# The opening of a two-layer decoder trunk: token statistics by single-column products, c as one row, other orders of transfer

## The chip, the cores and the metric

The kernel runs on one core of a Trainium2 chip. The core has a tensor engine (PE, with its weight loads shown apart as PEld), VectorE (DVE), ScalarE (ACT), GpSimd (POOL) and SyncE (SP), which here only issues transfers. Each works through its own queue in order, and they meet through semaphores. The metric is the device time of one execution in microseconds (us), the median of several runs.

## The reference

Two layers; in each an adaptive layer norm, a mixer block and a feed-forward block. What matters here is the very start:

```python
c_act = jax.nn.silu(c)                                   # c: (1, 1024)
mod = (c_act @ w_ada + b_ada)[:, None, :]                # six parts of 1024
sh1, sc1, g1, sh2, sc2, g2 = jnp.split(mod, 6, axis=-1)
h = rmsnorm(x, norm1_w) * (1 + sc1) + sh1                # x: (1, 512, 1024) f32
u = h @ w_in
...
def rmsnorm(x, w):
    xf = xf * lax.rsqrt(jnp.mean(xf * xf, axis=-1, keepdims=True) + EPS)
    return xf.astype(x.dtype) * w
```

All is fp32. The mean runs over the 1024 features of each of the 512 tokens.

## The kernel before

Activations lie with features on partitions: `x[k]`, k = 0 to 7, is a tile of 128 features by 512 tokens. A product of full accuracy is three products of split operands (`mm3`, L156): each operand is split into a rounded part `hi`, made on ScalarE, and the rest `lo`, made on DVE. Weights arrive by SyncE as `raw` tiles (`fetch`, L229), ScalarE makes `whi` (L322) and DVE makes `wlo` (L325).

**The opening.** ScalarE's queue loads c, already spread over 128 partitions by the host (512 KB, L184), and the columns `colt`; SyncE loads the eight x tiles (256 KB each, L187) and behind them, per tile k, the weights of the scale part SC1 and of the shift part SH1 (512 KB each, `ada_first_load`, L374), then `raw` tiles. A dot of such weights with `csil`, the silu of c, is one DVE pass over 128x1024 (`ada_dot`, L371); ScalarE turns its sum into a column of `amod` or `mod` (L388, L391).

For the statistics DVE and ScalarE square the x tiles (L725, L727), DVE adds them in pairs (L729), and PE multiplies each pair's sum by a tile of ones (L730), which leaves the sum over features in all 128 partitions, 128x512. The root comes from ScalarE (L737) and three DVE passes over 128x512 improve it by a newton step (L738 to L740) into `norm.rstd`.

**The first input tiles.** Tile k of h is made in three steps: `first_scaled` (x times scale column times rstd, DVE, L490), `first_hi` (plus shift column, rounded, ScalarE, L494) and `first_lo` (DVE, L497). With `hi`, `lo`, `whi` and `wlo` of tile k PE does 21 products of 512 columns for that k (L787, L789); k runs from 0 to 7 with seven sums open at once. From k=2 on, the step for k+2 is written ahead of the products of k.

**What sets the order.** `pin` and `matmul` keep DVE's and PE's instructions in the order of the code. ScalarE's and SyncE's are placed by the scheduler that builds the program, by its own idea of when operands are there. Products of ones by ones (`WARM`, 22 of them, at the start; `WARM2`, 16, ahead of the main work) have no result that is used.

Of the kernel before, what the change touches and what calls it, by code (L numbers as in the profile page):

```python
# [12 lines left out]
F32 = mybir.dt.float32  # L13
F32R = mybir.dt.float32r
I32 = mybir.dt.int32
AF = mybir.ActivationFunctionType
ALU = mybir.AluOpType
# [3 lines left out]
P = 128  # L21
D = 1024
S = 512
L = 2
KT = D // P
# [3 lines left out]
TT = S // P  # L29
# [5 lines left out]
BLOCK = 256  # L35
DFF = 2816
NF = DFF // P
EPS = 1e-6
# [18 lines left out]
SH1, SC1, G1, SH2, SC2, G2 = range(6)  # L57
# [9 lines left out]

WARM = 22

WARM2 = 16  # L70

GATE2 = ([("gate", j) for j in range(6)] + [("attn", 0), ("attn", 1), ("gate", 6), ("gate", 7)]
         + [("attn", j) for j in range(2, 8)])
# [3 lines left out]
def hybrid_trunk(ctx, tc, xT, ws, ada, cols, pool_w, qk_w, crow, pos, con, out):  # L77
    nc = tc.nc
    V, A, T = nc.vector, nc.scalar, nc.tensor
# [14 lines left out]
    def bigt(dt=F32R):  # L94
        return big.tile([P, S], dt, tag="big", name=nm("big"))
# [4 lines left out]
    def ps_mm():  # L100
        return psum.tile([P, S], F32, tag="mm", name=nm("mm"), bufs=4)
# [7 lines left out]
    def sm(shape, dt=F32, tag="sm", bufs=8):  # L109
        return small.tile(shape, dt, tag=tag, name=nm(tag), bufs=bufs)  # L110
# [36 lines left out]
    def matmul(*a, **k):  # L147
        tc.keep_in_program_order(T.matmul(*a, **k))  # L148

    def pin(ins):  # L150
        return tc.keep_in_program_order(ins)
# [16 lines left out]

    def table(func, after):

        A.activation(sm([P, 1], tag="tab", bufs=1), after, func)

    blank = const.tile([P, 1], F32, name="blank")
    V.memset(blank, 0.0)
# [3 lines left out]
    x = [const.tile([P, S], F32, name=f"x{k}") for k in range(KT)]  # L178
# [2 lines left out]
    qkw = const.tile([P, L, 2, ROPE], F32, name="qkw")  # L181
    post = const.tile([P, TT], I32, name="post")
    csil = const.tile([P, D], F32, name="csil")
    A.dma_start(csil, crow)  # L184
    A.dma_start(colt, cols)
    for k in range(KT):
        nc.sync.dma_start(x[k], xT[k * P:(k + 1) * P, :])  # L187

    INV, M4, M16 = cont[:, 0:2], cont[:, 2:3], cont[:, 3:4]
# [3 lines left out]
    ident = const.tile([P, P], F32, name="ident")  # L193
    make_identity(nc, ident)
    ones = const.tile([P, P], F32, name="ones")
# [5 lines left out]
    epst = const.tile([P, 1], F32, name="epst")  # L201
    nc.gpsimd.memset(epst, EPS)

    A.activation(csil, csil, AF.Silu)

# [121 lines left out]
    def load_w():  # L329
        while at[1] < min(at[0] + 1 + SUMS_AHEAD, len(items)):  # L330
            sums, sub = items[at[1]]
            if sums is not None and sub == 0:
                sums.begin()
            at[1] += 1
        sums, what = items[at[0]]
        at[0] += 1
        if sums is not None:
            return sums.load(what)
        l, blocks = what
        raw = rawt()  # L340
        fetch(raw, l, blocks)
        return split_w(raw, len(blocks))
# [28 lines left out]
        return V.scalar_tensor_tensor(aw, aw, 1.0, csil, op0=ALU.mult, op1=ALU.mult,  # L371
                                      accum_out=mod[l][:, part, j:j + 1])

    def ada_first_load(j):  # L374
        tiles = {}
        for part in (SC1, SH1):
            tiles[part] = w4([P, D])
            nc.sync.dma_start(tiles[part], ada[0, part, j])
        return tiles
# [4 lines left out]
    def ada_first(j, tiles, part):  # L384
        pin(ada_dot(tiles[part], 0, part, j))
        m = mod[0][:, part, j:j + 1]
        if part == SC1:
            A.activation(amod[0][0][:, j:j + 1], m, AF.Identity, scale=colt[:, 0, C_N1 + j:C_N1 + j + 1],  # L388
                         bias=abias[:, j:j + 1])
        else:  # L390
            A.activation(m, m, AF.Identity, bias=colt[:, 0, C_ADA + part * KT + j:C_ADA + part * KT + j + 1])  # L391
# [47 lines left out]
    class Norm:  # L439
# [44 lines left out]
                A.activation(self.h[k][:, lo:hi], t[:, lo:hi], AF.Identity, bias=sh)  # L484
            return ins

        def first_scaled(self, k):

            self.t = tmp()
            pin(V.scalar_tensor_tensor(self.t, x[k], amod[0][0][:, k:k + 1], self.rstd,  # L490
                                       op0=ALU.mult, op1=ALU.mult))

        def first_hi(self, k):
            A.activation(self.hi[k], self.t, AF.Identity, bias=mod[0][:, SH1, k:k + 1])  # L494
# [80 lines left out]
    def cell(n):  # L575
        return sm([P, 2 * n], tag="asm", bufs=16)
# [137 lines left out]
    scratch = ps_pair()  # L714
    norm = Norm()
    for _ in range(WARM):
        matmul(scratch[:, 1, :P], ones, ones, start=True, stop=True)
    table(AF.Abs_reciprocal_sqrt, csil[:, 0:1])
    first = [ada_first_load(0)]
    pin(V.scalar_tensor_tensor(abias, colt[:, 0, C_ADA + SC1 * KT:C_ADA + (SC1 + 1) * KT], 1.0,  # L720
                               colt[:, 0, C_N1:C_N1 + KT], op0=ALU.add, op1=ALU.mult))
    sq = [bigt(F32) for _ in range(KT)]
    for k in range(KT):
        if k == 0 or (k % 2 == 1 and k < KT - 1):
            pin(V.tensor_mul(sq[k], x[k], x[k]))  # L725
        else:
            A.activation(sq[k], x[k], AF.Square)  # L727
        if k % 2 == 1:
            pin(V.tensor_add(sq[k], sq[k - 1], sq[k]))  # L729
            matmul(scratch[:, 0], ones, sq[k], start=(k == 1), stop=(k == KT - 1))  # L730
    idle = ps_mm()
    for _ in range(WARM2):
        matmul(idle[:, :P], ones, ones, start=True, stop=True)
    ada_first(0, first[0], SC1)
    ada_first(0, first[0], SH1)
    y, t = bigt(F32), bigt(F32)
    A.activation(y, scratch[:, 0], AF.Abs_reciprocal_sqrt, bias=epst, scale=1.0 / D)  # L737
    pin(V.scalar_tensor_tensor(t, scratch[:, 0], D * EPS, y, op0=ALU.add, op1=ALU.mult))  # L738
    pin(V.scalar_tensor_tensor(t, t, -0.5 / D, y, op0=ALU.mult, op1=ALU.mult))
    pin(V.scalar_tensor_tensor(norm.rstd, t, 1.5, y, op0=ALU.add, op1=ALU.mult))  # L740
    norm.first_scaled(0)
    norm.first_hi(0)
    loaded.append(load_w())
    norm.first_lo(0)
    first.append(ada_first_load(1))
# [11 lines left out]
    for l in range(L):  # L757
# [317 lines left out]
        norm = n2  # L1075
# [229 lines left out]
```

## Time and profile before

| | us |
|---|---|
| median of three runs | 1459.17 |
| their range | 1458.58 to 1460.15 |
| the profiled execution | 1460.31 |
| its span, first to last instruction | 1458.5 |
| PE busy in the span | 1443.1 (99%) |
| DVE busy | 1049.3 (72%) |
| ACT busy | 677.0 (46%) |

The profiled execution lasts 1.8 us longer than its span. Matmul records overlap and their ends are modelled, so the busy share of PE says that it was never left without work, not how fast that work went. The chain of waits is followed back from the last instruction, at each step to what released it; its pieces carry a start and a length. Idle time of an engine counts only where the chain goes through it.

### The profile page before, as it was taken

The page shows a single profiled execution, that of the slowest core. Times are in us where ns is not written, and L with a number is a line of the kernel's source. Part 1 is how long each engine was busy: PE and PEld are TensorE (multiplying, and loading weights), DVE is VectorE, ACT ScalarE, POOL GpSimd, SP SyncE. Part 2 cuts the span into 40 slices and gives each one's busy share as a digit, 9 for nine tenths or more (in the row PEclk, how much of TensorE's full clock was granted, in tenths as well). Part 3 has the DMA queues.
Part 4 walks back from the last instruction along what each step waited for, and adds up shares of the span by engine and source line. Part 5 has one row for each costly group of instructions (what it writes and reads, how often), then busy time and mean ns, then how long its engine had stood idle before and what let it go on. Part 6 is the DMA issues. An engine that isn't in the chain of part 4 may idle for free.

```text
span 1458.5 us, 21780 instructions
## 1 busy us (share of the span) xinstructions
PE 1443.1 (99%) x8379; PEld 1263.7 (87%) x8379; DVE 1049.3 (72%) x1831; ACT 677.0 (46%) x1202; POOL 106.9 (7%) x156
## 2 busy tenths in 40 slices
PE   9999999999999999999999999999999999999999
PEld 7888787888989998989998878888889889989997
DVE  7987778748786767677677867675487756657673
ACT  4635555543553452535444355555335525434451
POOL 0000000010001120211000000001000102111100
PEclk9999999999999999999999999999999999999999
DMA  9654333464337666675436522224452445736532
GB/s 350 212 168 161 125 116 116 146 172 166 98 120 217 183 181 221 164 217 140 135 99 216 186 98 78 73 73 134 118 185 72 128 136 147 195 102 178 147 107 74
DMA packets 84407, 217.16 MB, mean 149 GB/s; under 512 B 10832, under 2 KB 23760, under 8 KB 84304
## 3 DMA queue, kind: packets, MB, share of 16 engines
q1 hardware_dynamic: 67456, 177.37, 36.8%
q0 software_dynamic: 16128, 37.76, 11.9%
q8 instruction: 65, 1.06, 0.3%
q10 hardware_dynamic: 720, 0.66, 0.1%
q14 instruction: 38, 0.31, 0.1%
HBM read 213.65 MB, written 2.10 MB: 148 GB/s over the span
## 4 chain that ended last, share of the span: by engine, by line
PE 88%; DVE 5%; DMA 3%; ACT 2%; issue 1%; SPq 0%; ACTq 0%; DVEq 0%
PE mm L148 74%; PE pair L148 12%; DMA dot<-in_ada 2%; PE pair L154 1%; DMA raw<-in_ws 1%; DVE wlo L325 1%; ACT whi L322 1%; DVE dot L371 1%; PE mm L154 0%; ACT tmp L584 0%; DMA w<-in_ada 0%; DMA x<-in_xT 0%; DVE w L371 0%; DVE big L508 0%; DVE tmp L478 0%
## 5 line engine op out<-in xcount | busy, mean ns | idle before, releaser
L148 PE MATMUL mm<-big,whi 128*128 128x512 f32 (+1 forms) x4362 | 1078.9, 339 | 1.9 <-DVE big L508 0.8
L148 PEld LDWEIGHTS mm<-big,whi 128*128 128x128 f32 x4362 | 747.6, 190 | 87.5 <-DVE big L508 1.2
L148 PE MATMUL mm<-big,wlo 128*128 128x512 f32 (+1 forms) x2181 | 736.0, 337 | 1.7 <-DVE wlo L325 1.7
L148 PEld LDWEIGHTS mm<-big,wlo 128*128 128x128 f32 x2181 | 413.9, 190 | 46.5 <-DVE wlo L325 2.6
L322 ACT ACTIVATE whi<-raw 128x1024 fp32r<-128x1024 f32 (+2 forms) x240 | 248.6, 1038 | 350.0 <-PE mm L148 253.9
L325 DVE TENSOR_TENSOR wlo<-raw,whi 128x1024 fp32r<-128x1024 f32 (+2 forms) x240 | 285.0, 1194 | 60.6 <-ACT whi L322 60.3
L322 ACT ACTIVATE whi<-w 128x1024 fp32r<-128x1024 f32 x72 | 76.3, 1060 | 123.9 <-PE mm L148 83.3
L371 DVE SCALAR_TENSOR_TENSOR dot<-dot,csil 128x1024 f32<-128x1024 f32 x80 | 96.8, 1222 | 33.4 <-DMA dot<-in_ada 33.3
L251 POOL DMA_DIRECT2D w<-in_ws x72 | 49.2, 689 | 928.6 <-DVE wlo L325 667.1
L1000 DVE SCALAR_TENSOR_TENSOR x<-mm,mod,x 128x512 f32<-128x512 f32 (+1 forms) x90 | 61.4, 689 | 74.0 <-PE mm L148 74.0
L325 DVE TENSOR_TENSOR wlo<-w,whi 128x1024 fp32r<-128x1024 f32 x72 | 87.2, 1218 | 0.0
L253 POOL DMA_DIRECT2D w<-in_ws x72 | 64.3, 927 | 196.4 <-DMA w<-in_ws 166.4
L148 PE MATMUL pair<-whi,big 128*128 128x512 f32 x224 | 76.7, 390 | 0.0
L148 PE MATMUL pair<-big,whi 128*128 128x256 f32 (+1 forms) x376 | 74.8, 294 | 0.0
L148 PEld LDWEIGHTS pair<-big,whi 128*128 128x128 f32 x376 | 60.4, 191 | 2.2
L148 PE MATMUL mm<-whi,big 128*128 128x512 f32 x160 | 57.2, 394 | 1.7 <-ACT big L494 1.4
L584 ACT ACTIVATE tmp<-pair,asm,nrq 128x256 f32<-128x256 f32 (+1 forms) x96 | 49.5, 527 | 16.4 <-DVE asm L676 16.0
L148 PE MATMUL pair<-big,wlo 128*128 128x256 f32 (+1 forms) x188 | 55.3, 294 | 0.0
L960 DVE SCALAR_TENSOR_TENSOR big<-big,mm 128x512 f32<-128x512 f32 x48 | 32.6, 684 | 29.9 <-PE mm L148 29.4
L148 PEld LDWEIGHTS pair<-whi,big 128*128 128x128 f32 x224 | 42.1, 188 | 8.7
L508 DVE TENSOR_TENSOR big<-tmp,big 128x512 fp32r<-128x512 f32 x48 | 32.8, 690 | 18.7 <-ACT big L507 18.7
L599 ACT ACTIVATE w<-pair 128x512 fp32r<-128x512 f32 (+2 forms) x48 | 25.2, 525 | 44.5 <-PE pair L154 26.2
(183 smaller groups left out, 1236.6 us busy)
## 6 DMA issues: line engine op xcount, KB each, us to landing
raw<-in_ws SPq DMA_DIRECT2D x146, 512.0 KB, 3.4
dot<-in_ada SPq DMA_DIRECT2D x80, 512.0 KB, 4.2
w<-in_ws POOLq DMA_DIRECT2D x144, 256.0 KB, 4.7
raw<-in_ws SPq DMA_DIRECT2D x64, 256.0 KB, 3.9
raw<-in_ws SPq DMA_DIRECT2D x24, 384.0 KB, 3.4
w<-in_ada SPq DMA_DIRECT2D x16, 512.0 KB, 5.8
raw<-in_ws SPq DMA_DIRECT2D x16, 448.0 KB, 5.0
raw<-in_ws SPq DMA_DIRECT2D x36, 128.0 KB, 3.9
```

The source lines that it names most:

```text
L148: tc.keep_in_program_order(T.matmul(*a, **k))
L154: tc.keep_in_program_order(T.transpose(*a))
L251: nc.gpsimd.dma_start(dst, self.source(0, 1))
L253: nc.gpsimd.dma_start(dst, self.source(*other), accum_op=ALU.add)
L322: A.activation(hi[:, :n], raw[:, :n], AF.Copy)
L325: ins = V.tensor_sub(lo[:, :n], raw[:, :n], f32(hi)[:, :n])
L371: return V.scalar_tensor_tensor(aw, aw, 1.0, csil, op0=ALU.mult, op1=ALU.mult, accum_out=mod[l][:, part, j:j + 1])
L508: V.tensor_sub(lo, src, f32(hi))
L584: A.activation(out, s, AF.Exp, bias=bias, scale=scale, accum_out=den)
L599: A.activation(both[:, :, :, 0], tp, AF.Copy)
L960: V.scalar_tensor_tensor(sg, sg, 1.0, branch, op0=ALU.add, op1=ALU.mult)
L1000: V.scalar_tensor_tensor(x[k][:, lo:hi], src, mod[l][:, part, k:k + 1], x[k][:, lo:hi], op0=ALU.mult, op1=ALU.add)
```

## The change

The statistics are made with tokens on partitions. The squares of tile k become the *weights* of four products per k with one column of ones as the moving operand; each gives a 128x1 column of sums for 128 tokens, and over all k a 128x4 tile `st`. The root and the newton step work on 128x4. To bring the result back to rows, DVE multiplies the identity by the four columns (`diag`), and a product of ones with it gives `rows`, 128x512, in PSUM. The first scaling reads `rows`; ScalarE copies them to `norm.rstd` for the later ones.

Only one row of c is loaded (4 KB) and put through silu; two products of a row of ones with it spread it over the partitions, and DVE copies both halves to `csil`. SyncE loads x 0 to 3, the scale weights, x 4 to 7, the shift weights. Six squares are on ScalarE and two on DVE; the pair sums are gone. The scale dot of k=0 stands amid the squares, the shift dot behind the diagonal. `WARM2` is 14.

```diff
-WARM2 = 16
+WARM2 = 14
+HALF_X = 4
...
-    A.dma_start(csil, crow)
+    A.dma_start(csil[0:1], crow[0:1])
     A.dma_start(colt, cols)
-    for k in range(KT):
+    for k in range(HALF_X):
         nc.sync.dma_start(x[k], xT[k * P:(k + 1) * P, :])
...
-    A.activation(csil, csil, AF.Silu)
+    A.activation(csil[0:1], csil[0:1], AF.Silu)
...
-    first = [ada_first_load(0)]
+    first = [ada_first_load(0, (SC1,))]
+    for k in range(HALF_X, KT):
+        nc.sync.dma_start(x[k], xT[k * P:(k + 1) * P, :])
+    first[0].update(ada_first_load(0, (SH1,)))
...
-    for k in range(KT):
-        if k == 0 or (k % 2 == 1 and k < KT - 1):
+    st = ps_mm()[:, :TT]
+    def square(k):
+        if k < 2:
             pin(V.tensor_mul(sq[k], x[k], x[k]))
         else:
             A.activation(sq[k], x[k], AF.Square)
-        if k % 2 == 1:
-            pin(V.tensor_add(sq[k], sq[k - 1], sq[k]))
-            matmul(scratch[:, 0], ones, sq[k], start=(k == 1), stop=(k == KT - 1))
-    idle = ps_mm()
+    def square_sums(k):
+        for t in range(TT):
+            matmul(st[:, t:t + 1], sq[k][:, t * P:(t + 1) * P], ones[:, 0:1], start=(k == 0 and t == 0),
+                   stop=(k == KT - 1), skip_group_check=True)
+    spread = [ps_mm(), ps_mm()]
+    for k in range(2):
+        square(k)
+    for h in range(2):
+        matmul(spread[h], ones[0:1], csil[0:1, h * S:(h + 1) * S], start=True, stop=True)
+    for k in range(2):
+        square_sums(k)
+    for h in range(2):
+        pin(V.tensor_copy(csil[:, h * S:(h + 1) * S], spread[h]))
+    for k in range(2, KT):
+        square(k)
+        if k == 4:
+            ada_first(0, first[0], SC1)
+        square_sums(k)
+    y, t, r = cell(2), cell(2), cell(2)
+    A.activation(y, st, AF.Abs_reciprocal_sqrt, bias=epst, scale=1.0 / D)
+    pin(V.scalar_tensor_tensor(t, st, D * EPS, y, op0=ALU.add, op1=ALU.mult))
+    pin(V.scalar_tensor_tensor(t, t, -0.5 / D, y, op0=ALU.mult, op1=ALU.mult))
+    pin(V.scalar_tensor_tensor(r, t, 1.5, y, op0=ALU.add, op1=ALU.mult))
+    diag = bigt(F32).rearrange("p (t q) -> p t q", q=P)
+    rows = ps_mm()
+    for h in range(2):
+        ts = slice(2 * h, 2 * h + 2)
+        pin(V.tensor_mul(diag[:, ts], ident.unsqueeze(1).to_broadcast([P, 2, P]),
+                         r[:, ts].unsqueeze(2).to_broadcast([P, 2, P])))
+        matmul(rows[:, h * BLOCK:(h + 1) * BLOCK], ones, diag[:, ts].rearrange("p t q -> p (t q)"),
+               start=(h == 0), stop=True, skip_group_check=True)
     for _ in range(WARM2):
-        matmul(idle[:, :P], ones, ones, start=True, stop=True)
-    ada_first(0, first[0], SC1)
+        matmul(scratch[:, 1, :P], ones, ones, start=True, stop=True)
     ada_first(0, first[0], SH1)
-    y, t = bigt(F32), bigt(F32)
-    A.activation(y, scratch[:, 0], AF.Abs_reciprocal_sqrt, bias=epst, scale=1.0 / D)
-    pin(V.scalar_tensor_tensor(t, scratch[:, 0], D * EPS, y, op0=ALU.add, op1=ALU.mult))
-    pin(V.scalar_tensor_tensor(t, t, -0.5 / D, y, op0=ALU.mult, op1=ALU.mult))
-    pin(V.scalar_tensor_tensor(norm.rstd, t, 1.5, y, op0=ALU.add, op1=ALU.mult))
-    norm.first_scaled(0)
+    norm.first_scaled(0, rows)
     norm.first_hi(0)
+    A.activation(norm.rstd, rows, AF.Copy)
```

Three places in the built programs. PE's queue at the start, before (`pair_124` is the PSUM tile of the sums, `big` here are squares, `mm_260` is the first main sum):

```order
L148 MATMUL pair_124<-ones 128x128 x22
L148 MATMUL pair_124<-big_174,ones 128x512
L148 MATMUL pair_124<-big_176,ones 128x512
L148 MATMUL pair_124<-big_178,ones 128x512
L148 MATMUL pair_124<-big_180,ones 128x512
L148 MATMUL mm_197<-ones 128x128 x16
L148 MATMUL mm_260<-whi_229,big_128 128x512
```

The same place in the changed program (`mm_182` and `mm_183` are the spread halves of c, `mm_173` is `st`, `mm_238` is `rows`):

```order
L150 MATMUL pair_120<-ones 128x128 x22
L150 MATMUL mm_182<-csil,ones 128x512
L150 MATMUL mm_183<-csil,ones 128x512
L150 MATMUL mm_173<-ones,big_174 128x1 x4
L150 MATMUL mm_173<-ones,big_175 128x1 x4
...
L150 MATMUL mm_173<-ones,big_181 128x1 x4
L150 MATMUL mm_238<-big_237,ones 128x256 x2
L150 MATMUL pair_120<-ones 128x128 x14
L150 MATMUL mm_296<-whi_265,big_124 128x512
```

Four products of 512 columns became two of 512 for c, 32 of one column and two of 256.

DVE from the last square to the first scaling, before:

```order
L729 TENSOR_TENSOR big_180<-big_179,big_180 128x512
L371 SCALAR_TENSOR_TENSOR w_168,mod_115<-w_168,csil 128x1024
L371 SCALAR_TENSOR_TENSOR w_170,mod_115<-w_170,csil 128x1024
L738 SCALAR_TENSOR_TENSOR big_219<-pair_124,big_218 128x512
L739 SCALAR_TENSOR_TENSOR big_219<-big_219,big_218 128x512
L740 SCALAR_TENSOR_TENSOR big_127<-big_219,big_218 128x512
L490 SCALAR_TENSOR_TENSOR tmp_224<-x_77,am_117,big_127 128x512
```

And in the changed program (`asm` are 128x4 tiles, `big_237` is the diagonal):

```order
L732 TENSOR_TENSOR big_175<-x_78 128x512
L749 COPY csil<-mm_182 128x512
L749 COPY csil<-mm_183 128x512
L373 SCALAR_TENSOR_TENSOR w_164,mod_111<-w_164,csil 128x1024
L757 SCALAR_TENSOR_TENSOR asm_231<-mm_173,asm_230 128x4
L758 SCALAR_TENSOR_TENSOR asm_231<-asm_231,asm_230 128x4
L759 SCALAR_TENSOR_TENSOR asm_232<-asm_231,asm_230 128x4
L764 TENSOR_TENSOR big_237<-ident,asm_232 128x256 x2
L373 SCALAR_TENSOR_TENSOR w_170,mod_111<-w_170,csil 128x1024
L492 SCALAR_TENSOR_TENSOR tmp_259<-x_77,am_113,mm_238 128x512
```

The shift dot moved from ahead of the statistics to a place between the diagonal and the first scaling.

ScalarE around the tiles k=1 and k=2, before (`whi_277` is the weights' high part for k=2, `big_130` the high part of h for k=2):

```order
L391 ACTIVATE mod_115<-mod_115,colt 128x1
L494 ACTIVATE big_129<-tmp_240,mod_115 128x512
L388 ACTIVATE am_117<-mod_115,abias,colt 128x1
L391 ACTIVATE mod_115<-mod_115,colt 128x1
L322 ACTIVATE whi_277<-raw_275 128x896
L494 ACTIVATE big_130<-tmp_272,mod_115 128x512
```

And in the changed program (there `whi_313` and `big_126`):

```order
L393 ACTIVATE mod_111<-mod_111,colt 128x1
L496 ACTIVATE big_125<-tmp_276,mod_111 128x512
L390 ACTIVATE am_113<-mod_111,abias,colt 128x1
L393 ACTIVATE mod_111<-mod_111,colt 128x1
L496 ACTIVATE big_126<-tmp_308,mod_111 128x512
L324 ACTIVATE whi_313<-raw_311 128x896
```

For k=2 the two large passes changed places. From k=3 to the end of the program every queue holds the same operations in the same order as before.

## Rows read from the trace of the kernel before

**Rows 1.** Windows: length, busy us and count by engine, clock, DMA share, GB/s.

```profile
17.70:29.20 11.50, 11.15 (x45) 8.03 (x45) 10.39 (x17) 4.50 (x8) 0.00 (x0) 1.00 1.02 402
29.20:54.00 24.80, 24.80 (x109) 20.56 (x110) 24.63 (x37) 13.26 (x23) 0.00 (x0) 1.00 0.78 268
54.00:1458.50 1404.50, 1392.58 (x8143) 1223.56 (x8141) 1002.90 (x1761) 649.96 (x1158) 105.58 (x146) 1.00 0.48 142
```

**Rows 2.** Chain of waits of the first 40 us: start, length, what.

```profile
6.80 5.95 DMA w<-in_ada
...
12.78 1.23 DVE w L371 x2
...
16.11 0.03 DVE tmp L490
...
29.19 0.50 PE mm L148
```

**Rows 3.** Timelines and groups of PE and PEld, opening; groups: busy us, mean ns.

```profile
1.13 6.79 PE L148 MATMUL pair<-ones 128*128 128x128 f32 x44 [1.13 <-POOL ones L196]
...
7.99 0.30 PEld L148 LDWEIGHTS pair<-big,ones 128*128 128x128 f32 x2 [0.27 <-DVE big L729]
...
12.62 3.62 PE L148 MATMUL mm<-ones 128*128 128x128 f32 x31
...
12.19 0.59 PE L148 MATMUL pair<-big,ones 128*128 128x512 f32 x1
12.62 0.27 PE L148 MATMUL mm<-ones 128*128 128x128 f32 x1
...
17.73 0.50 PE L148 MATMUL mm<-whi,big 128*128 128x512 f32 x1 [1.37 <-ACT big L494]
...
L148 PEld LDWEIGHTS pair<-big,ones 128*128 128x128 f32 x8 | 1.3, 188 | 3.0 <-DVE big L729 2.8
...
L148 PE MATMUL mm<-ones 128*128 128x128 f32 x32 | 3.7, 275 | 0.0
```

**Rows 4.** Timeline of PEld: the first two loads of six transposes.

```profile
141.96 0.14 PEld L154 LDWEIGHTS pair<-ident,tmp 128*128 128x128 f32 x1 [0.25 <-issue]
...
142.01 0.14 PEld L154 LDWEIGHTS pair<-ident,tmp 128*128 128x128 f32 x1
```

**Rows 5.** Timeline of PE, 2 to 4 us: six records each, the 2.79 record in both.

```profile
1.72 1.49 PE L148 MATMUL pair<-ones 128*128 128x128 f32 x6
...
2.79 1.49 PE L148 MATMUL pair<-ones 128*128 128x128 f32 x6
```

**Rows 6.** Timeline of ACT and DVE in the opening; L827's durations min/median/max in ns.

```profile
5.84 0.17 DVE L720 SCALAR_TENSOR_TENSOR abias<-colt 128x8 f32<-128x8 f32 x1 [4.98 <-DMA colt<-in_cols]
...
7.21 0.20 ACT L171 ACTIVATE tab<-csil 128x1 f32<-128x1 f32 x1
...
9.39 1.29 ACT L727 ACTIVATE big<-x 128x512 f32<-128x512 f32 x2 [0.77 <-DMA x<-in_xT]
...
12.63 0.39 ACT L388 ACTIVATE am<-mod,abias,colt 128x1 f32<-128x1 f32 x1 [1.94 <-DVE w L371]
...
12.92 0.67 ACT L737 ACTIVATE big<-pair,epst 128x512 f32<-128x512 f32 x1
...
13.93 0.69 DVE L738 SCALAR_TENSOR_TENSOR big<-pair,big 128x512 f32<-128x512 f32 x1
...
L827 DVE TENSOR_TENSOR pwl<-tmp,pwh x2: 416/416/417, 67.5 to 791.7; 128x256 fp32r<-128x256 f32 x2
```

**Rows 7.** Timeline of ACT and DVE around tile k=2.

```profile
26.09 0.75 DVE L490 SCALAR_TENSOR_TENSOR tmp<-x,am,big 128x512 f32<-128x512 f32 x1
...
26.41 0.94 ACT L322 ACTIVATE whi<-raw 128x896 fp32r<-128x896 f32 x1
...
27.25 0.71 ACT L494 ACTIVATE big<-tmp,mod 128x512 fp32r<-128x512 f32 x1
27.38 1.09 DVE L325 TENSOR_TENSOR wlo<-raw,whi 128x896 fp32r<-128x896 f32 x1 [0.54 <-ACT whi L322]
```

More of the change, by code (lines that the diff above doesn't have):

```diff
@@ L169, in table @@
     def table(func, after):
-        A.activation(sm([P, 1], tag="tab", bufs=1), after, func)
+        A.activation(sm([P, 1], tag="tab", bufs=1)[:after.shape[0]], after, func)
     blank = const.tile([P, 1], F32, name="blank")
@@ L372, in ada_dot, with ada_first_load @@
                                       accum_out=mod[l][:, part, j:j + 1])
-    def ada_first_load(j):
+    def ada_first_load(j, parts=(SC1, SH1)):
         tiles = {}
-        for part in (SC1, SH1):
+        for part in parts:
             tiles[part] = w4([P, D])
@@ L485, in apply, with first_scaled @@
             return ins
-        def first_scaled(self, k):
+        def first_scaled(self, k, rstd=None):
             self.t = tmp()
-            pin(V.scalar_tensor_tensor(self.t, x[k], amod[0][0][:, k:k + 1], self.rstd,
-                                       op0=ALU.mult, op1=ALU.mult))
+            pin(V.scalar_tensor_tensor(self.t, x[k], amod[0][0][:, k:k + 1],
+                                       self.rstd if rstd is None else rstd, op0=ALU.mult, op1=ALU.mult))
         def first_hi(self, k):
@@ L717, in hybrid_trunk @@
         matmul(scratch[:, 1, :P], ones, ones, start=True, stop=True)
-    table(AF.Abs_reciprocal_sqrt, csil[:, 0:1])
-    first = [ada_first_load(0)]
+    table(AF.Abs_reciprocal_sqrt, csil[0:1, 0:1])
+    first = [ada_first_load(0, (SC1,))]
+    for k in range(HALF_X, KT):
+        nc.sync.dma_start(x[k], xT[k * P:(k + 1) * P, :])
+    first[0].update(ada_first_load(0, (SH1,)))
     pin(V.scalar_tensor_tensor(abias, colt[:, 0, C_ADA + SC1 * KT:C_ADA + (SC1 + 1) * KT], 1.0,
                                colt[:, 0, C_N1:C_N1 + KT], op0=ALU.add, op1=ALU.mult))
+    st = ps_mm()[:, :TT]
     sq = [bigt(F32) for _ in range(KT)]
-    for k in range(KT):
-        if k == 0 or (k % 2 == 1 and k < KT - 1):
+    def square(k):
+        if k < 2:
             pin(V.tensor_mul(sq[k], x[k], x[k]))
```

## The prediction

> **What bounds the kernel now.** The windows come first: from 29.2 us to the end the tensor engine (PE) is busy for 24.80 of 24.80 us and 1392.58 of 1404.50 us, and the granted clock is 1.00, the 2.4 GHz level [rows 1]. So the kernel is bound by PE, and a change in the opening is worth what it moves the moment from which PE runs full; nothing later hands it back. In the chain of waits that moment is 29.19, the third product of input tile k=2 [rows 2]. Before it the chain hangs on VectorE (DVE): the shift weights land at 12.75 (6.80 + 5.95), the two dots follow, then three passes of the newton step over 128x512, and the first scaling starts at 16.11 [rows 2, 6]. From there DVE works almost without a hole, tile after tile. PE's own part is small: four products of 512 columns, then the warm-up products, and it waits. So I ask two things: when can the first scaling start in the changed kernel (16.11 now), and how long from there to the third product of k=2 (29.19 - 16.11 = 13.08 us now).
>
> **What the change saves.** c comes as one row of 4 KB in place of 512 KB, so about 1.3 us of transfer at the 402 GB/s of [rows 1] leaves the queue, and the shift weights should land near 11.4. The three newton passes of 0.69 shrink to 128x4. Two squares on DVE and all pair sums go; ScalarE has six squares, the last of them for an x tile that lands as late as before (as many bytes stand ahead of it: the scale weights take c's place), so it ends near 10.7 (9.39 + 1.29) [rows 6]. All of that is early work that must then meet PE.
>
> **What it puts on PE: the step that decides.** PE works its queue in order: 22 warm-up products, two spreading products of 512 columns, 32 single-column products, two products of 256, 14 warm-ups, the main work.
> - An fp32 product is two records in the trace (22 products, 44 records). The last warm-up record starts at 1.13 + 6.79 - 0.28 = 7.64, so the spread can begin at 7.75 [rows 3].
> - Records of 512 columns stand 12.62 - 12.19 = 0.43 us apart. Four of them: 1.72 us, to 9.47. These here have one row of weights, which no row of the trace shows; I take the same streaming time (were they free, all that follows would come 1.7 earlier, which is inside my range).
> - A single-column product holds the squares as weights, 128x128 fp32, so each of its two records loads a fresh tile. What such a load costs when nothing hides it is in the trace: of two loads that take 0.30 together and 0.188 each, the second starts 0.11 after the first [rows 3]. Records of 128 columns, which load a tile each too, stand (3.62 - 0.275) / 30 = 0.1115 apart. Bounds: below, the 0.05 us between the first two loads of transposes [rows 4], another form of load; above, the 0.214 (five steps from 1.72 to 2.79) of the same records early in the opening, twice the spacing, which I read as the 1.2 GHz level [rows 5]. I take 0.1115: same type, same loads, same clock.
> - 32 products x 2 records x 0.1115 = 7.14 us, to 16.61; the last one drains 0.16 more (0.275 - 0.1115): 16.77. The sums stood at 12.78 before (12.19 + 0.59). PE, which had slack, is now 4 us late, long after the last square.
>
> The Trainium skill, page "TensorE: Matmul & The Clock Gate", section "LDWEIGHTS (loading the stationary operand)", gives columns / 1.2 ns, 107 ns for 128 columns, whatever the rows; the trace agrees with 0.11. The same page under "Back-to-back issue gap" gives 1 to 64 columns some 60 cycles, 25 ns. By that alone the 64 records would take an estimated 1.6 us; it leaves the load out.
>
> **From the sums to the first scaling.** ScalarE takes 0.14 to start (12.78 to 12.92); on 128x4 I put 0.25, between the 0.20 of a 128x1 and the 0.67 of a 128x512, near the first. Three DVE steps of 0.17 (the 128x8 row) with 0.03 between: 0.60. The diagonal, two 128x256 products of 0.416 that overlap by 0.07: 0.68 until the next can start. Then the shift dot stands in DVE's queue ahead of the scaling: 1.15 (12.78 to 13.93) [rows 2, 6]. In sum 16.77 + 0.14 + 0.25 + 0.03 + 0.60 + 0.68 + 1.15 = 19.62, or 3.51 later than 16.11. The spreading by ones (half two: 18.55 + 0.15 + two records of 0.21 and the drain, 19.3) is hidden by that dot. Behind the dot on DVE waits everything, and SyncE's in-order queue too: a later transfer reuses the shift dot's buffer and is issued near 19.6, with the raw weights of k=2 behind it. They are not needed before 30 and had 10 us of backlog ahead of them before that will be gone; I cost it at nothing.
>
> **From the scaling to 29.19.** DVE's order is the same from here, so each step shifts by 3.51, but one place on ScalarE is new: for k=2 the split of the weights (whi) now stands behind the high half of h. Before: whi 26.41, h 27.25, and DVE's wlo already waits 0.54 and starts at 27.38 [rows 7]. Now: scaling ends 26.84, h from 26.94 to 27.65, whi from about 27.6 to 28.53, wlo at 28.56, all plus 3.51: 1.18 more. DVE needs about 4.65 us per tile (two dots of 1.15 and passes of 0.75, 1.09 and 0.75, each less an overlap of 0.08) and PE 21 products at 24.80 / 109 = 0.2275 [rows 1], 4.8 us, so PE is not stopped again, nor does it regain. PE itself: warm-ups from 19.1 for 28 x 0.1115 = 3.12 to 22.25, two tiles and two products, 10.0, would be ready at 32.2; that is hidden by up to 1.6 us behind 33.88. The copy of the rstd rows on ScalarE (some 0.67) falls into a hole before the next dot ends. The third product of k=2 comes at 29.19 + 3.51 + 1.18 = 33.88: **+4.7 us**.
>
> Against the profiled execution (1460.31, its span 1458.5) that is 1465.0. The median of the three runs is 1459.17, 1.14 under it, so **1463.9**.
>
> **Rivals.**
> 1. *Single columns are nearly free* (the other side: not slower). If the loads were pulled under one another, the sums would wait for the squares (10.7) and for ScalarE, where the scale column of k=0 stands ahead of the root: copies of 0.69 from 9.64 (8.78 for the first) to 10.35, dot to 11.6, 0.39 for the column, so 12.0 [rows 6]. Then 12.0 + 0.28 + 0.60 + 0.68 + 1.15 = 14.7 for the scaling, 1.4 earlier; with the 1.18 on ScalarE -0.2: 1459.0. This holds under 0.035 us a record; with the transposes' 0.05 it is +0.8 to +1.1, 1460.3. The gain is gone at 0.04, and from 0.084 the kernel is slower by over 0.2%. Against it: the 0.11 of an unhidden fp32 load. For it: nothing in this trace has a single column.
> 2. *The clock falls.* During the sums the array gets one column per load for 7 us. Nothing in this trace is like that: PE was idle for 1.4 us before 17.73 and its next stretch has a granted clock of 1.00 [rows 1, 3], that is all. If it falls with a quarter of the records left, 16 x 0.10 = 1.6 us more; the 28 warm-up records then take up to 6.0 in place of 3.1 and the spreading 0.5 more, so PE is ready at 27.3 + 10.0 = 37.3, +8.1 (with the clock back midway, +6.7). Falling at the very end costs +5.5, halfway +9. I take +7.5: 1466.7. The same page, section "Part 4: PE-mode transpose", says that transposes don't count as a busy PE in the same way; no run shows yet what single columns count as.
> 3. *The swap on ScalarE costs nothing*: only the 3.5 us remain, 1462.7. Part of the forecast's own spread.
>
> **How the numbers follow.** The forecast with its spread (+2.5 to +5.5, rival 3 in it) has 0.50, the falling clock 0.25, nearly free columns 0.20; 0.05 is for a gain that I don't see. Less than 0.2%, 2.9 us, is about what a measurement of this kernel can't tell from no change. Slower: 0.47 of the forecast and all of the clock, 0.72; within: 0.20 + 0.03 = 0.23; faster: 0.05. The range reaches from 1460.0 (0.05 us a record) to 1468.0 (clock lost before the last quarter); left out are the free columns, the unseen gain and the worst of the clock, some 0.2.
>
> **What will show it.** Right: single-column records 0.11 apart, the root on 128x4 near 16.9, the first scaling near 19.6, DVE's wlo of k=2 waiting some 1.7 us for whi, the third product of k=2 near 33.9, all later stretches as long as before. A spacing well under 0.08, or 0.21 with warm-ups at the low level, makes rival 1 or 2 true. I am wrong altogether if the first main product comes before 19 or if PE is not full behind k=2.

## The result and the profile after

| | before | after |
| --- | --- | --- |
| median of the runs, us | 1459.66 (4 runs) | 1470.27 (4 runs, 1469.51 to 1470.59) |
| ratio, 95% interval | | 1.0072 [1.0059, 1.0085] |
| span of the profiled execution, us | 1458.5 | 1467.7 |
| mean granted clock | 1.0 | 0.995 |
| sums complete on PE, us | 12.78 | 22.14 |
| first scaling on DVE starts | 16.11 | 25.80 |
| third product of k=2 starts | 29.19 | 40.04 |

The kernel became 10.6 us slower. The forecast had the direction and 4.7 us, and 1470.27 lies outside the range of 1460 to 1468. From the third product of k=2 to the end the spans are 1429.3 us before and 1467.7 - 40.04 = 1427.7 after, so all of the loss stands ahead of that product, as the prediction assumed: +10.85 there. (The 1.6 us between these two rests say nothing: in the profiles of all the kernels below the rest lasts 1426.2 to 1433.2 us.)

The windows of the opening, in the columns of [rows 1], show where.

```profile
8.00:12.00 4.00, 4.00 (x24) 2.63 (x22) 1.86 (x3) 2.52 (x4) 0.00 (x0) 1.00 1.04 404
12.00:16.00 4.00, 4.00 (x26) 4.00 (x26) 0.76 (x2) 0.39 (x1) 0.00 (x0) 0.66 1.03 396
16.00:20.00 4.00, 4.00 (x20) 4.00 (x20) 0.00 (x0) 0.00 (x0) 0.00 (x0) 0.50 1.00 394
20.00:24.00 4.00, 2.46 (x12) 2.37 (x12) 1.28 (x6) 1.10 (x2) 0.00 (x0) 0.50 0.05 22
24.00:28.00 4.00, 4.00 (x20) 3.64 (x20) 3.31 (x5) 1.50 (x3) 0.00 (x0) 0.63 0.46 142
28.00:32.00 4.00, 4.00 (x26) 3.52 (x25) 3.54 (x7) 1.49 (x3) 0.00 (x0) 1.00 0.64 225
```

Read the column behind POOL, the granted clock: 1.00, then 0.66, 0.50, 0.50, 0.63, 1.00. From about 13.3 to 26.9 us PE has the 1.2 GHz level. It counts as busy for 4.00 of 4.00 us when the clock falls and up to 20 us, and from 16 to 20 us DVE and ACT have 0 instructions: both wait for the sums.

The timeline of PE in the same stretch (start, length, what, count, idle time before; it answers to [rows 3]):

```profile
1.14 7.72 PE L150 MATMUL pair<-ones 128*128 128x128 f32 x44 [1.14 <-POOL ones L198]
...
8.78 1.98 PE L150 MATMUL mm<-csil,ones 1*128 1x512 f32 x4
10.69 11.45 PE L150 MATMUL mm<-ones,big 128*128 128x1 f32 x64
23.68 2.08 PE L150 MATMUL mm<-big,ones 128*128 128x256 f32 x4 [1.54 <-DVE big L764]
25.55 3.97 PE L150 MATMUL pair<-ones 128*128 128x128 f32 x28
29.28 0.48 PE L150 MATMUL mm<-whi,big 128*128 128x512 f32 x1
...
40.04 0.50 PE L150 MATMUL mm<-whi,big 128*128 128x512 f32 x1 [0.16 <-DVE big L499]
```

The last row is the third product of k=2. The 64 single-column records take 11.45 us where 7.14 and a drain of 0.16 were forecast. Grouped over the first part of them (10.65 to 13.2 us) and over the last (13.4 to 22.2 us; a record at the border counts in both), with busy time and mean of one:

```profile
L150 PE MATMUL mm<-ones,big 128*128 128x1 f32 x23 | 2.7, 251 | 0.0
...
L150 PE MATMUL mm<-ones,big 128*128 128x1 f32 x42 | 9.0, 349 | 0.0
```

At the high level 23 records lie in 2.7 us, (2.7 - 0.25) / 22 = 0.11 apart; at the low level 42 lie in 9.0 us, (9.0 - 0.35) / 41 = 0.21 apart. The forecast spacing was right, and then the clock doubled it.

The rows of DVE and ACT behind the sums answer to [rows 6] and, the last three, to [rows 7]:

```profile
22.25 0.26 ACT L756 ACTIVATE asm<-mm,epst 128x4 f32<-128x4 f32 x1 [9.07 <-PE mm L150]
...
22.54 0.16 DVE L757 SCALAR_TENSOR_TENSOR asm<-mm,asm 128x4 f32<-128x4 f32 x1 [9.79 <-ACT asm L756]
...
23.88 1.22 DVE L373 SCALAR_TENSOR_TENSOR w<-w,csil 128x1024 f32<-128x1024 f32 x1
...
25.80 0.75 DVE L492 SCALAR_TENSOR_TENSOR tmp<-x,am,mm 128x512 f32<-128x512 f32 x1 [0.69 <-PE mm L150]
...
36.62 0.73 ACT L496 ACTIVATE big<-tmp,mod 128x512 fp32r<-128x512 f32 x1 [0.43 <-DVE tmp L492]
37.26 0.94 ACT L324 ACTIVATE whi<-raw 128x896 fp32r<-128x896 f32 x1
...
38.23 1.09 DVE L327 TENSOR_TENSOR wlo<-raw,whi 128x896 fp32r<-128x896 f32 x1 [1.70 <-ACT whi L324]
```

The root on 128x4 takes 0.26 (0.25 was put), each newton step 0.16 (0.17), and the split of k=2 waits 1.70 for whi (1.7). New is the 0.69 ahead of the first scaling: the two 256-column products run at the low level (2.08 us), so the rstd rows come after the shift dot and not behind its cover.

### The profile page after: what moved, and what is told of

Same layout as the page of the kernel before. It is cut to its first block, busy times and chain, and to the rows that moved or that the text cites. A ratio compares the mean times of both kernels' runs of the same rounds, so it can differ in the third digit from the quotient of the medians.

```text
span 1467.7 us, 21902 instructions
## 1 busy us (share of the span) xinstructions
PE 1453.7 (99%) x8439; PEld 1277.1 (87%) x8439; DVE 1045.9 (71%) x1829; ACT 678.8 (46%) x1205; POOL 106.8 (7%) x156
## 4 chain that ended last, share of the span: by engine, by line
PE 92%; DVE 4%; ACT 2%; DMA 1%; issue 1%; SPq 0%; POOL 0%; ACTq 0%; DVEq 0%; POOLq 0%
PE mm L150 77%; PE pair L150 13%; PE pair L156 1%; DMA dot<-in_ada 1%; DVE wlo L327 1%; ACT whi L324 1%; DVE dot L373 1%; PE mm L156 0%; DMA raw<-in_ws 0%; ACT tmp L586 0%; DVE w L373 0%; DVE tmp L480 0%; ACT w L541 0%; DVE big L499 0%; DVE tmp L623 0%
```

## Experiments

The theory: the products that move one column for each weight load bring the clock back to 1.2 GHz, though PE counts as busy throughout. Rivals: something else in the new opening lowers it (the one-row products, the gaps around them); and, for the rest of the loss, the exchanged order of whi and h on ScalarE costs nothing. Medians stand against runs of the kernel before on the same chip.

| kernel | median, us | before | ratio, 95% | mean clock, all runs | first scaling | third of k=2 |
| --- | --- | --- | --- | --- | --- | --- |
| after | 1470.27 | 1459.66 | 1.0072 [1.0059, 1.0085] | 0.994 to 0.995 | 25.80 | 40.04 |
| e1, 128 columns | 1465.81 | 1460.43 | 1.0041 [1.0027, 1.0055] | 1.0 | 20.94 | 35.18 |
| e2, c whole | 1465.68 | 1460.43 | 1.0034 [1.0021, 1.0047] | 0.996 to 0.997 | 21.77 | 36.00 |
| e4, order | 1471.04 | 1460.43 | 1.0076 [1.0053, 1.0099] | 0.993 to 0.995 | 25.80 | 39.69 |
| e5, 128 columns and order | 1465.33 | 1460.43 | 1.0032 [1.0021, 1.0043] | 0.999 to 1.0 | 20.44 | 33.52 |
| e6, half the products | 1464.08 | 1460.32 | 1.0028 [1.0018, 1.0038] | 0.995 to 0.997 | 20.03 | 34.72 |
| e3, row alone | 1460.85 | 1460.32 | 1.0002 [0.9992, 1.0012] | 1.0 | 17.21 | 29.95 |
| e8, early spread, wide | 1461.48 | 1460.32 | 1.0005 [0.9995, 1.0014] | 0.999 to 1.0 | 20.65 | 33.72 |
| e9, early spread | 1462.08 | 1460.32 | 1.0018 [1.0008, 1.0029] | 0.998 to 1.0 | 17.96 | 30.69 |
| e10, e9 with 128 rows | 1459.52 | 1460.08 | 0.9999 [0.9988, 1.0009] | 0.999 to 1.0 | 16.36 | 29.07 |
| e11, e8 with 128 rows | 1459.39 | 1460.08 | 0.9995 [0.9987, 1.0004] | 0.999 to 1.0 | 17.09 | 30.16 |
| e12, e10 less warm-up | 1459.26 | 1459.91 | 0.9994 [0.9984, 1.0005] | 0.997 to 1.0 | 15.12 | 28.85 |
| e13, e11 less warm-up | 1459.45 | 1459.91 | 0.9998 [0.9988, 1.0008] | 0.998 to 1.0 | 14.81 | 27.89 |

**e1: 128 columns in place of one.**

```diff
-    st = ps_mm()[:, :TT]
+    stw = ps_mm().rearrange("p (t q) -> p t q", q=P)
+    st = stw[:, :, 0]
...
-            matmul(st[:, t:t + 1], sq[k][:, t * P:(t + 1) * P], ones[:, 0:1], start=(k == 0 and t == 0),
+            matmul(stw[:, t], sq[k][:, t * P:(t + 1) * P], ones, start=(k == 0 and t == 0),
```

The run also pins ScalarE's two passes of k=2 in the order that they have in after, so that only the number of columns differs.

> After, with one thing changed: the products of the statistics move 128 columns of ones instead of one, so each fills a whole bank and the first column of each is read; loads, their number and all that follows are the same. Theory T (the clock falls because the array receives one column a load for some 7 us): the granted clock stays at 1.0 through the opening, records stay 0.11 us apart, the sums end near 18.0 us (after: 22.1), the first scaling starts near 20.9 (after: 25.8), the third product of k=2 near 35.1 (after: 40.0), and the kernel takes some 1465.6 us. Rival R1 (the fall comes from what lies before the sums, the one-row products of the spread and the gaps around them): the clock falls at 13 us as in after, and the time is that of after, 1470.

Timelines of PE and DVE:

```profile
10.65 7.41 PE L150 MATMUL mm<-ones,big 128*128 128x128 f32 x64
19.60 1.13 PE L150 MATMUL mm<-big,ones 128*128 128x256 f32 x4 [1.54 <-DVE big L769]
...
20.94 0.74 DVE L494 SCALAR_TENSOR_TENSOR tmp<-x,am,mm 128x512 f32<-128x512 f32 x1
...
35.18 0.49 PE L150 MATMUL mm<-whi,big 128*128 128x512 f32 x1 [0.16 <-DVE big L503]
```

and its windows:

```profile
12.00:16.00 4.00, 4.00 (x39) 4.00 (x37) 0.72 (x2) 1.34 (x2) 0.00 (x0) 1.00 1.04 402
16.00:20.00 4.00, 2.46 (x21) 2.23 (x20) 1.37 (x6) 1.10 (x2) 0.00 (x0) 1.00 0.98 388
```

128 times as many columns, and 4 us less: 64 records in 7.41 us at a clock of 1.00. The clock stayed at 1.0 in all five runs and was lowered in all four of after. The loads, their number, the spread and the gaps around it are the same in both, so the one-column products lower the clock, and R1 falls here. The first scaling comes 4.86 us earlier than in after, the third product of k=2 4.86 as well. That is the price of the clock, but for the 0.04 us by which the sums begin earlier (10.65 against 10.69). It shows a second thing too: at the high level a record costs the same with 1 column as with 128. So the columns do not set the 0.11; that the fresh load sets it, which both have, fits but is argued.

**e2: c whole, no spread.** The one-row products and the two copies are gone, the single columns stay.

```diff
-    A.dma_start(csil[0:1], crow[0:1])
+    A.dma_start(csil, crow)
...
-    for h in range(2):
-        matmul(spread[h], ones[0:1], csil[0:1, h * S:(h + 1) * S], start=True, stop=True)
...
-    for h in range(2):
-        pin(V.tensor_copy(csil[:, h * S:(h + 1) * S], spread[h]))
```

> After, with c loaded as 128 rows as in the kernel before and silu taken of the whole, so the products that spread the row and the copies behind them are gone; the single-column products stay. Theory T: the sums begin near 8.2 us, and the clock falls all the same, some 2.5 to 5 us into them, so that they end at 17.5 to 20 us. Rival R1 (the spread's one-row products or the gaps around them let the clock fall): it stays at 1.0, and the sums end near 15.5 us.

The timeline of PE in e2:

```profile
8.20 9.92 PE L150 MATMUL mm<-ones,big 128*128 128x1 f32 x64
```

and its windows:

```profile
8.00:12.00 4.00, 4.00 (x39) 4.00 (x37) 1.23 (x2) 2.94 (x7) 0.00 (x0) 1.00 1.00 374
12.00:16.00 4.00, 4.00 (x22) 4.00 (x22) 0.00 (x0) 0.20 (x1) 0.00 (x0) 0.54 1.03 409
```

With no one-row product and no gap ahead of them (PE goes from the warm-ups straight into the sums) the clock falls all the same, in the profile near 12 us (0.54 from 12 to 16); its mean is 0.996 to 0.997 in all five runs. The sums end at 8.20 + 9.92 = 18.12, inside what was expected. Together e1 and e2 show that the fall needs the single columns and does not need the one-row products or the gap. How many columns are enough, and whether single columns with weights that stay do the same, no run shows.

**e6: 16 products in place of 32** (the pair sums of the kernel before put back on DVE).

> After with the pair sums back on VectorE, so 16 single-column products in place of 32; all else as after, the changed order of whi and h for k=2 included or not is left to the scheduler, which here keeps whi ahead. Theory T (each record 0.11 at the high level, and the clock falls only some us after the single columns begin): 32 records take 3.6 us, less what waits for the last squares; the sums end near 14.5 to 15.5 us, the clock falls little or not at all before, the first scaling comes at 17.5 to 18.5 us and the kernel takes 1.5 to 3.5 us more than before. If the clock falls as early relative to the sums' begin and stays down for the main work, the warm-ups and the first main products show 0.21 spacing and it is 4 us or more.

The timeline of PE in e6:

```profile
10.68 1.05 PE L150 MATMUL mm<-ones,big 128*128 128x1 f32 x8
12.13 4.26 PE L150 MATMUL mm<-ones,big 128*128 128x1 f32 x24 [0.40 <-DVE big L753]
```

and its windows:

```profile
12.00:16.00 4.00, 3.87 (x23) 3.87 (x24) 2.42 (x5) 0.39 (x1) 0.00 (x0) 0.66 1.04 389
...
20.00:24.00 4.00, 4.00 (x22) 4.00 (x22) 3.55 (x5) 2.42 (x4) 0.00 (x0) 0.56 0.75 240
```

A miss on the size. Half the records did not spare the clock: 0.66 from 12 to 16 us, and still 0.56 from 20 to 24, where the warm-ups run. The sums ended at 12.13 + 4.26 = 16.39, the first scaling came at 20.03 against 17.5 to 18.5, and 3.8 us were lost against the kernel before. (Here the scheduler keeps whi ahead of h for k=2, so the third product is not to be set against that of after.)

**e4 and e5: whi ahead of h for k=2 again,** in after and in e1. Both pin the two instructions and write k=2's load ahead of its `first_hi`:

```diff
-                    norm.first_hi(k + 2)
+                    if k > 0:
+                        norm.first_hi(k + 2)
                 loaded.append(load_w())
+                if k == 0:
+                    norm.first_hi(k + 2)
```

> After, with only the order of ScalarE's two rounding copies of k=2 put back (whi ahead of h). Theory T: wlo of k=2 waits 0.5 us for whi instead of 1.7, and the third product of k=2 starts near 39.3 us instead of 40.0, there held by PE itself, so 0.75 us less than after. Rival R3: no change from after.

> As the run with 128 columns, and the two rounding copies of k=2 on ScalarE in the order of the kernel before (whi ahead of h). Theory T: the opening as in that run, the third product of k=2 near 34.0 us, some 1464.5 us, 1.1 less than that run. Rival R3 (the order on ScalarE costs nothing, since PE isn't ready earlier): the third product at the same time as in that run.

The timelines of DVE, ACT and PE, first of e4, then of e5:

```profile
37.07 1.09 DVE L329 TENSOR_TENSOR wlo<-raw,whi 128x896 fp32r<-128x896 f32 x1 [0.54 <-ACT whi L324]
...
39.69 0.39 PE L150 MATMUL mm<-whi,big 128*128 128x512 f32 x1
```

```profile
31.71 1.09 DVE L329 TENSOR_TENSOR wlo<-raw,whi 128x896 fp32r<-128x896 f32 x1 [0.54 <-ACT whi L324]
...
37.04 0.95 ACT L324 ACTIVATE whi<-raw 128x896 fp32r<-128x896 f32 x1 [0.95 <-DMA raw<-in_ws]
...
33.52 0.50 PE L150 MATMUL mm<-whi,big 128*128 128x512 f32 x1
...
38.66 0.50 PE L150 MATMUL mm<-whi,big 128*128 128x512 f32 x1 [0.53 <-ACT big L498]
```

The wait of wlo falls from 1.70 to 0.54 in both, so the mechanism is as priced (1.16 of the 1.18). What reaches PE differs. In e4 the third product comes 0.35 earlier instead of 0.75: PE itself holds it there, the row has no idle time ahead of it, and the first main product of that run came 0.30 later (29.58). In e5 it comes 1.66 earlier than in e1, 0.50 of which its first scaling already had. But one tile later part is handed back: whi of k=4 stands ahead of h of k=3 on ScalarE and waits 0.95 for its transfer, and PE waits 0.53 for that h. In the medians neither shows: e4 is 0.8 above after, which ran at another time, and e5 is 0.5 under e1.

**e3: the row alone.** The statistics of the kernel before are put back; the row, its spread, after's order of transfers and the six squares on ScalarE stay.

> After without its single-column products: c comes as a row and is spread by the two products, transfers in after's order, six squares on ScalarE, but pair sums on VectorE, four products of 512 columns for the sums, and the newton step over 128x512 as in the kernel before. The order of whi and h for k=2 on ScalarE is that of the kernel before too. Theory T: the granted clock stays at 1.0; VectorE now has the two copies (0.69 each) and the two dots amid the pair sums, so its first scaling comes near 17.6 to 18.4 us (before: 16.1), the third product of k=2 near 30.7 to 31.5, 1.5 to 2.3 over the kernel before. Rival R1 (the spread's products lower the clock): a fall of the clock as in after.

The timeline of ACT in e3, behind the sums:

```profile
13.29 0.95 ACT L324 ACTIVATE whi<-raw 128x896 fp32r<-128x896 f32 x1 [0.84 <-DMA raw<-in_ws]
14.15 0.28 ACT L393 ACTIVATE mod<-mod,colt 128x1 f32<-128x1 f32 x1
14.33 0.67 ACT L749 ACTIVATE big<-pair,epst 128x512 f32<-128x512 f32 x1
```

The clock stays at 1.0, the first scaling comes 1.1 late and the third product 0.76 late, less than expected, and the time is that of before. So the row brings no gain here, though its transfer is shorter: the last product of the sums is done at 13.81, but the root stands behind whi on ScalarE and waits until 14.33. So the loss belongs to the new statistics and the exchanged order: of the medians, e1 - e3 is 5.0 us (64 records at the high level, what stands behind them, and the order) and after - e1 another 4.5 (the clock; 4.9 in the traces).

**e8 and e9: the spread among the warm-ups.** To use the shorter transfer, the spread was put behind 8 of the 22 warm-up products and all x tiles ahead of the weights. e9 keeps the statistics of before, e8 has pair sums, 16 products of 128 columns and the newton step on 128x4. Both also put ScalarE's root ahead of other work there.

```diff
-    for _ in range(WARM):
+    for _ in range(WARM1):
+        matmul(scratch[:, 1, :P], ones, ones, start=True, stop=True)
+    spread = [ps_mm(), ps_mm()]
+    for h in range(2):
+        matmul(spread[h], ones[0:1], csil[0:1, h * S:(h + 1) * S], start=True, stop=True)
+    for _ in range(WARM - WARM1):
         matmul(scratch[:, 1, :P], ones, ones, start=True, stop=True)
```

> A version built on what the runs showed: c as a row, spread by products that stand behind 8 of the 22 warm-up products, the copies right behind the first pair sum; all x tiles ahead of both weights as in the kernel before; pair sums on VectorE, 16 products that move 128 columns of ones (not one), the newton step on 128x4 and the diagonal as in after, dots before and behind it; whi ahead of h for k=2. Theory T: clock at 1.0 throughout, shift weights land near 11.4 us, sums end near 11.3, first scaling near 14.1 (before: 16.1), third product of k=2 near 27.2 to 28 (before: 29.2), so 1 to 2 us faster than the kernel before. Rival: raw weights land too late for the earlier start, or VectorE's other work takes the gain, and it is within 0.5 us of before.

> The kernel before with only c as a row, spread behind 8 of the 22 warm-up products and copied behind the first pair sum, two squares on VectorE and six on ScalarE; the statistics and the order of transfers as in the kernel before, ScalarE's root ahead of the shift column of k=0. Theory T: everything that waits for transfers comes 1.3 us earlier: shift weights land near 11.4 us, first scaling near 14.7 (before: 16.1), third product of k=2 near 27.8 to 28, 1.2 to 1.4 us faster than before. Rival: the two copies crowd VectorE as in the run with the row alone, and there is no gain.

Both missed: e8 is 1.2 us above the kernel before, within its interval, and e9 is 1.8 us slower. The timeline of PE in e8, then that of e9:

```profile
4.85 3.78 PE L152 MATMUL mm<-csil,ones 1*128 1x512 f32 x4
8.56 5.64 PE L152 MATMUL pair<-ones 128*128 128x128 f32 x28
```

```profile
4.59 1.98 PE L150 MATMUL mm<-csil,ones 1*128 1x512 f32 x4
6.50 5.02 PE L150 MATMUL pair<-ones 128*128 128x128 f32 x28
11.36 3.60 PE L150 MATMUL pair<-big,ones 128*128 128x512 f32 x8
```

and its windows:

```profile
4.00:8.00 4.00, 4.00 (x21) 2.63 (x20) 3.49 (x7) 3.41 (x6) 0.00 (x0) 0.96 0.98 342
8.00:12.00 4.00, 4.00 (x20) 3.75 (x20) 3.34 (x6) 1.93 (x4) 0.00 (x0) 0.61 1.04 422
```

28 warm-up records last 3.29 us at the high level. In e9 they last 5.02, because the clock, already risen, falls again (0.61 from 8 to 12 us). In e8 they last 5.64 and the one-row products 3.78 instead of 1.98: by the spacing of its records its clock had not yet risen. Its clock column reads 1.00 in that stretch all the same, as it does in [rows 5]'s stretch of before, whose records are 0.214 apart too; so early the spacing of the records is the better witness. The sums then ended at 17.8 us in e8 and 15.0 in e9.

**e10 and e11: the same with 128 rows.** silu is written to the first row of two tiles that DVE has set to zero, and the spread products take all 128 rows. e11 also puts the root ahead of the scale column of k=0.

```diff
+    for h in range(2):
+        V.memset(crows[h], 0.0)
+        A.activation(crows[h][0:1], csil[0:1, h * S:(h + 1) * S], AF.Silu)
...
-        matmul(spread[h], ones[0:1], csil[0:1, h * S:(h + 1) * S], start=True, stop=True)
+        matmul(spread[h], ones, crows[h], start=True, stop=True)
```

> As the kernel before with the row early, with one difference: the silu of the row is written to the first row of two tiles of 128x512 that VectorE has set to zero, so the four spreading records load 128 rows of weights' worth of moving data instead of one, at the same place and with the same number of columns. Theory T2 (what lowered the clock in that run, from 7.6 to 11.0 us, are the products with one row; it is not the place of the spread or the gaps around it): the granted clock rises before 6 us and stays, the 28 warm-up records behind the spread end near 9.4 us, the sums near 11.2, the first scaling comes near 15.0 (before: 16.1), the third product of k=2 near 28.1 (29.2), 1 us faster than the kernel before. Rival R4 (the place or the gaps): the clock falls again between 7 and 11 us, and the time is 1462 as with one row.

> The same spread over 128 rows in the kernel with pair sums, 16 products that move 128 columns, the newton step on 128x4 and the diagonal; ScalarE's root now ahead of the scale column of k=0. Theory T2: the clock stays at 1.0 from its rise on, sums end near 11.5 us, first scaling near 14.4 to 14.7 (before: 16.1), third product of k=2 near 27.5 to 28, 1.2 to 1.7 us faster than the kernel before. Rival R4: the clock rises only near 14 us as with one row, 1461.5 as there.

The timeline of PE in e10:

```profile
4.71 2.09 PE L150 MATMUL mm<-big,ones 128*128 128x512 f32 x4
6.64 3.29 PE L150 MATMUL pair<-ones 128*128 128x128 f32 x28
9.76 3.60 PE L150 MATMUL pair<-big,ones 128*128 128x512 f32 x8
```

and its windows:

```profile
8.00:12.00 4.00, 4.00 (x24) 2.81 (x23) 3.60 (x7) 1.93 (x4) 0.00 (x0) 1.00 1.04 420
```

In both the clock rises and stays up through the opening; the 28 records take 3.29. That speaks for T2, with one profile of each kernel, and the medians go the same way (e9 1.8 us above before, e10 0.6 under; e8 1.2 above, e11 0.7 under); in e12 and e13, built on them, the warm-ups behind the spread run at the high level too. But in e1 and e3 one-row products behind all 22 warm-ups lowered nothing, so they did harm only early, and what the place adds is left open. The forecast gain failed on PE's own queue: the sums stand behind the warm-ups and begin at 9.76, so that their eight records of 0.43 end at 13.36; in e11 they begin at 10.47. The first scalings came at 16.36 and 17.09, where 15.0 and 14.4 to 14.7 were expected.

**e12 and e13: 4 warm-up products behind the spread instead of 14** (`WARM = 12`).

> The kernel before with the row spread over 128 rows of weights, and 4 instead of 14 warm-up products behind the spread. In the run with 14 the sums could begin only at 9.8 us, behind the warm-up records, and their eight records of 0.43 us took until 13.4. Theory (PE's own queue took the gain): the sums follow the pair sums again, end near 11.5 us, the root near 12.9, first scaling near 15.1 (before: 16.1), third product of k=2 near 28.0 (29.2): 1 us faster than the kernel before, 1459. Rival: with fewer warm-up products the clock falls or rises later, and the first scaling comes after 16.

> The kernel with the row spread over 128 rows, pair sums, 16 products that move 128 columns, the newton step on 128x4 and the diagonal, and 4 instead of 14 warm-up products behind the spread. Theory: sums end near 11.6 us (with 14: 14.2), root near 11.9, the newton step behind the scale dot at 12.0, first scaling near 14.4 (with 14: 17.1; before: 16.1), third product of k=2 near 27.5: 1.5 us faster than the kernel before. Rival: the clock falls or rises later for want of warm-up products, and there is no gain; or the end of the program takes it back, since this differs by less than 0.2%.

In e12 the first scaling came at 15.12, as expected, but behind PE's wait of 1.40 us before the main work the clock fell (0.79 from 16 to 24 us), and the third product came at 28.85, only 0.34 ahead of before. The kernel before has a wait of 1.37 us at that place and no fall, so what else it takes is open. In e13 there was no fall, and the first scaling came 0.4 later than expected; its timelines of PE and DVE:

```profile
8.11 3.82 PE L152 MATMUL mm<-ones,big 128*128 128x128 f32 x32
...
14.81 0.74 DVE L498 SCALAR_TENSOR_TENSOR tmp<-x,am,mm 128x512 f32<-128x512 f32 x1
...
27.89 0.50 PE L152 MATMUL mm<-whi,big 128*128 128x512 f32 x1
```

The opening is 1.3 us shorter than that of before, with the same ideas as the change: a row, small statistics, a diagonal. The whole kernel is not measurably faster (0.9998 [0.9988, 1.0008]). From the third product of k=2 to the end the profiled executions of all these kernels last 1426.2 to 1433.2 us, which is more than 1.3 apart. The clock has a share in that: from 480 to 490 us it is 0.92 in the profile of e4, 0.85 in e10 and 0.87 in e12, and 1.00 in before and after.

## Why the prediction was wrong

- **PE bound from k=2 on, nothing handed back**: right. +10.85 at that product, +10.6 in the median.
- **The step that failed** is the third point of "What it puts on PE": "I take 0.1115: same type, same loads, same clock". Type and loads held (0.11 at the high level; e1 shows that 128 columns cost no more than one), the clock did not. Some 42 of the 64 records ran at 0.21 (which bears out the 0.214 that the prediction took for the 1.2 GHz level); that added 11.45 - 7.14 - 0.16 = 4.15 us. And at the low level the two 256-column products lost the shift dot's cover: 3.66 us from the sums to the first scaling instead of 2.85. e1 puts the whole of it at 4.86.
- **The rival was named, its chance and size were too small.** "The clock falls" had 0.25 and +7.5 us, from a fall with a quarter of the records left. It fell with two thirds left. My own figure for "halfway" said +9, and the range cut it off as "the worst of the clock". Its path was not the one that ended last either: it had PE's own queue reach the third product at 37.3, behind slow warm-up products, but in after that product waited for DVE (0.16), as in the forecast, only later. No row spoke for the high level under one column a load; the forecast rested on a clock of 1.00 across 1.4 us of idle PE, which is another thing. With nothing in the trace on either side the two cases deserved like chances, and the range the whole of the worse one.
- **A term mis-sized**: the sums began at 10.69, not 9.47. 0.93 of this is the warm-ups, 7.72 us in place of 6.79. The same 44 records last 6.52 (e3) to 8.03 (e4) in the profiles of the kernels that begin with them, since the moment at which their spacing drops from 0.21 to 0.11 differs (near 4 us in e3, near 7 in e4); I took one profile's value as fixed. The rest is the spread, 1.91 us to the next record instead of 1.72, and the step to it.
- **Nearly free columns** (0.20): wrong. The spacing at the high level is the 0.11 that the loads have.
- **From the scaling to k=2**: 14.24 us against 33.88 - 19.62 = 14.26. e1, without the fall, has 14.24 as well. The 1.18 on ScalarE is confirmed by e4 and e5 as a wait of wlo. Against rival 3 (the order costs nothing) stands e5, where it moved the third product by 1.16; in after itself e4 gives back only 0.35, and no median shows it.
- **The first scaling without the clock**: e1 has 20.94 where 19.62 was forecast, and the sum of the terms, started at e1's 10.65, gives 20.8. Its third product stands 35.18 - 29.19 = 5.99 behind that of before, its median 5.4. So for the kernel that moves 128 columns the terms were right, but for the begin of the sums.
- **A late transfer, costed at nothing**: right for after, not in general. In e5, which starts earlier, the raw weights of k=4 hold ScalarE for 0.95 us.

## What to carry to other kernels

Here an fp32 product that moves one column took as long as one that moves 128, each with its own weights of 128x128, and PE counted as busy in the profile while its clock fell: if the weights change every time anyway, move a full tile of columns. Where a chain has slack on one engine, ask of the engine that takes the work over what its clock will be, not only how many instructions it gets. And when a state has no row in the trace, let the range hold both of its sides in full.

## What the runs showed of the hardware

- Single-column fp32 products: 0.11 us a record at the 2.4 GHz level and 0.21 at 1.2 GHz, two records a product; in after, e2, e4 and e6 the clock was lowered in every run (mean 0.993 to 0.997), with 128 columns in none of e1's (1.0).
- The Trainium skill, page "TensorE: Matmul & The Clock Gate", section "Part 4: PE-mode transpose", says that transposes do not bring the clock up. The trace of after shows something near it for ordinary products with one column, which let a clock fall that had risen: 0.50 in windows in which PE is busy 4.00 of 4.00 us.
- One row of weights costs what 128 rows cost: records of 512 columns lie 0.43 apart in the spread of e3 and e9 with one row and in the sums of e10 with 128, and the loads of after take as long (group of PEld, mean in ns).

```profile
L150 PEld LDWEIGHTS mm<-csil,ones 1*128 1x128 f32 x4 | 0.7, 184 | 0.6 <-issue 0.5
```

  Against 188 in [rows 3]. The same page, section "LDWEIGHTS (loading the stationary operand)", says that the load goes by columns and not by rows; the trace agrees.
- The first rise of the clock, read from the spacing of the records, is not fixed: the same 44 warm-up records take 6.52 to 8.03 us in eight profiles. An opening that hangs on PE starts that much earlier or later.
